# Input projections: the low part of every third weight tile made by ScalarE and an accumulating transfer instead of VectorE

## The chip, the core and the metric

The kernel runs on one core of one Trainium2 chip. The metric is device time in microseconds (us) of one execution. The engines are named as in the profile: PE is TensorE, PEld its weight loads, DVE VectorE, ACT ScalarE, POOL GpSimd, SP SyncE, which only issues transfers here.

## The reference, cut to what matters

The program is one encoder block over 256 tokens of 2048 channels. The change touches only the weights of the first product, `proj = h @ w_in`, and of that only the columns of the LRU branch and of the short convolution:

```
proj = jnp.einsum('bsd,dc->bsc', h, w_in)
lru_x, conv_x, conv_bg, conv_cg, g_lru, g_conv = jnp.split(proj, SPLIT_POINTS, axis=-1)
u = centred_dwconv(lru_x, lru_conv_w, lru_conv_b, LRU_CONV_LEFT)
...
v = centred_dwconv(conv_cg * conv_x, sc_conv_w, sc_conv_b, SHORT_CONV_LEFT)
```

All values are float32. `w_in` has 2048 rows and 12800 columns. `lru_x` takes the first 2560 columns, the three convolution inputs 2048 each, and the two gates `g_lru` and `g_conv` the last 4096. After that come two linear recurrences over the tokens, output products, a merge, a LayerNorm, an MLP of width 8192 and a second LayerNorm.

## The kernel before, in words

Every product is made in split precision. An operand is cut into a high part `hi`, which is the value cast to the type float32r that one pass of PE carries, and a low part `lo`, which is what the cast left over. With activations that are split likewise, the weight's high part meets both halves of the activations (one product over 512 columns, L137) and its low part the high half only (256 columns, L138). So one block of 128 by 128 weights costs two products, and a tile of eight blocks sixteen.

The weights come as tiles of 128 partitions by 1024 float32 (512 KB) in one long stream, `Weights`, in the order of their use. For each tile `load` does four things:

- it takes a raw buffer (tag `raw`, three of them) and a buffer each for `hi` and `lo` (six of each);
- SP issues the transfer from memory into `raw` (L85);
- ACT casts `raw` into `hi` (L66);
- DVE subtracts, `lo = raw - hi` (L67). This is the last reader of `raw`, so the raw buffer is free again behind it.

`take` keeps the stream up to five tiles ahead of the product that is emitted (`AHEAD = 5`). A scheduler then places the instructions of each engine in a fixed order. All engines run their own queue in that order, and a waiting instruction holds up what stands behind it in the same queue.

The input projections run in the order that the loop over the 20 heads at L531 writes down. For each head come one LRU block of columns (tiles named `l`, two per head), one gate product (tile `g`, half a tile, the recurrence's own weights) and two or three convolution blocks (tiles `c`, two each). Between them stands what is done with the products: L215 and L218 add the two halves of a PSUM bank, L258 and L260 are the LRU's convolution on DVE, L287 the gates' sigmoids on ACT, L289 and L309 two products of the recurrence on POOL, L304, L305 and L314 its exponentials, tangents and roots on ACT, L310 to L321 the rest of it with the scans on DVE. After the heads come the tiles `sg` of the two mixer gates, which have only L215, L218 and L367 behind them, and then the later layers.

Of the kernel before, what the change touches and what calls it, by code (L numbers as in the profile page):

```python
# [8 lines left out]
F32 = mybir.dt.float32  # L9
F32R = mybir.dt.float32r  # L10
AF = mybir.ActivationFunctionType
ALU = mybir.AluOpType
# [3 lines left out]
T = 256  # L16
# [21 lines left out]


class Job:  # L40
    """Weights' tiles that are taken from the stream, the products with them, and what is done with the products."""

    def __init__(self, specs, mm, post, chained=False):
        self.specs, self.mm, self.post, self.chained = specs, mm, post, chained
# [3 lines left out]
def block_kernel(ctx: ExitStack, tc: tile.TileContext, xT, x, par, w_in, w_gate, w_lru, w_conv, w_o, w1, w2,  # L48
                 ln1_g, ln1_b, b2, ln2_g, ln2_b, out):
    nc = tc.nc  # L50
# [7 lines left out]
    def bank_a(name):  # L58
        return psa.tile([P, 512], F32, tag="a", name=name)

    def bank_b(name):
        return psb.tile([P, 512], F32, tag="b", name=name)

    def split(raw, hi, lo):
        """raw = hi + lo, each with the mantissa that one pass of TensorE carries."""
        made = nc.scalar.copy(hi, raw)  # L66
        nc.vector.tensor_tensor(lo, raw, hi.bitcast(F32), op=ALU.subtract)  # L67
        return made

    class Weights:  # L70
        """All weights' tiles in the order of their use, loaded and split some tiles ahead of it."""

        def __init__(self):
            self.specs, self.tiles, self.taken = [], [], 0

        def alloc(self, name):
            raw = wp.tile([P, CH * P], F32, tag="raw", name=f"raw_{name}", bufs=3)
            hi = wp.tile([P, CH * P], F32R, tag="hi", name=f"hi_{name}", bufs=BUFS)
            lo = wp.tile([P, CH * P], F32R, tag="lo", name=f"lo_{name}", bufs=BUFS)
            return raw, hi, lo  # L80

        def load(self):
            src, n, name = self.specs[len(self.tiles)]
            raw, hi, lo = self.alloc(name)
            nc.sync.dma_start(raw[:, :n], src)  # L85
            split(raw[:, :n], hi[:, :n], lo[:, :n])
            self.tiles.append((hi, lo))

        def take(self, hold=False):
# [7 lines left out]
    stream = Weights()  # L97
# [5 lines left out]
        return par_sb[:, o : o + 1]  # L103

    def decay_scale():
        """-8 softplus(-lambda), with log1p by a Newton step on expm1(y) = 2 t / (1 - t), t = tanh(y / 2)."""
        n = 2 * HEADS
        o = PCOLS["lam"][0]
        lam = par_sb[:, o : o + n]
        tl = {k: cp.tile([P, n], F32, name=f"sp_{k}") for k in ("e", "y", "t", "r", "q")}  # L110
        e, y, t, r, q = (tl[k] for k in ("e", "y", "t", "r", "q"))
        c = cp.tile([P, n], F32, name="c_neg")
        cpos = cp.tile([P, n], F32, name="c_pos")
        nc.scalar.activation(e, lam, AF.Abs)
        nc.scalar.activation(e, e, AF.Exp, scale=-1.0)
        nc.scalar.activation(y, e, AF.Ln, bias=1.0)
        nc.scalar.activation(t, y, AF.Tanh, scale=0.5)
        nc.vector.tensor_scalar(r, t, -1.0, 1.0, op0=ALU.mult, op1=ALU.add)
        nc.vector.reciprocal(q, r)
        nc.vector.scalar_tensor_tensor(r, t, 2.0, q, op0=ALU.mult, op1=ALU.mult)  # L120
        nc.vector.tensor_tensor(t, r, e, op=ALU.subtract)
        nc.vector.tensor_scalar_add(q, e, 1.0)
        nc.vector.reciprocal(r, q)
        nc.vector.tensor_tensor(q, t, r, op=ALU.mult)
        nc.vector.tensor_tensor(r, y, q, op=ALU.subtract)
        nc.vector.tensor_scalar(t, lam, -1.0, 0.0, op0=ALU.mult, op1=ALU.max)
        nc.vector.tensor_tensor(y, t, r, op=ALU.add)
        nc.vector.tensor_scalar(c, y, -LRU_C, None, op0=ALU.mult)
        nc.vector.tensor_scalar(cpos, y, LRU_C, None, op0=ALU.mult)
        return c, cpos  # L130

    def mm_blocks(ps, hi, lo, k0, k, n, src, w0=0):
        """ps[:, :T] + ps[:, T:] = W.T @ (hi + lo): W's high part meets both parts, its low part the high one."""
        for i in range(k0, k0 + k):
            s = src(i)
            w = slice((i - k0 + w0) * P, (i - k0 + w0 + 1) * P)
            nc.tensor.matmul(ps, hi[:, w], s, start=i == 0, stop=False)  # L137
            nc.tensor.matmul(ps[:, :T], lo[:, w], s[:, :T], start=False, stop=i == n - 1)  # L138
# [12 lines left out]
        return Job(specs, mm, lambda: post(st["ps"]))  # L151

    def group_job(w, cs, nk, src, posts, name, after=None):
        """Some blocks of columns side by side, so that products can begin while their second operand is in the making."""
        st = {}
        cuts = [(k0, min(CH, nk - k0)) for k0 in range(0, nk, CH)]
        specs = [(w[c, :, k0 : k0 + k, :].rearrange("p k q -> p (k q)"), k * P, f"{name}{c}_{k0}") for k0, k in cuts for c in cs]

        def mm():
            st["ps"] = [bank_a(f"ps_{name}{c}") for c in cs]  # L160
            for k0, k in cuts:
                with tc.issue_after(after().ins) if after else nullcontext():
                    tiles = [stream.take() for _ in cs]
                for i in range(k):
                    for ps, (hi, lo) in zip(st["ps"], tiles):
                        mm_blocks(ps, hi, lo, k0 + i, 1, nk, src, i)

        def post():
            for ps, p in zip(st["ps"], posts):
                p(ps)  # L170

        return Job(specs, mm, post)

    def row_job(w, nk, src, post, name, tail=0, between=None):
        """Products with tokens on the output's partitions; over the last tiles one half of the tokens after the other."""
        st = {}
        n = nk // 2
        specs = [(w[i], 2 * 512, f"{name}_{i}") for i in range(n)]

        def products(ps, i, t, hi, lo):  # L180
            for kk in range(2):
                k = 2 * i + kk
                s = src(k)
                c = slice(kk * 512, (kk + 1) * 512)
                sh = s[:, t * P : (t + 1) * P]
                sl = s[:, T + t * P : T + (t + 1) * P]
                nc.tensor.matmul(ps[t], sh, hi[:, c], start=k == 0, stop=False)  # L187
                nc.tensor.matmul(ps[t], sh, lo[:, c], start=False, stop=False)  # L188
                nc.tensor.matmul(ps[t], sl, hi[:, c], start=False, stop=k == nk - 1)  # L189

        def mm():
            ps = st["ps"] = [bank_b(f"pr_{name}_{t}") for t in range(2)]
            for i in range(n - tail):
                hi, lo = stream.take()
                for t in range(2):
                    products(ps, i, t, hi, lo)
            last = [stream.take(between is not None and i > 2) for i in range(tail)]
            for t in range(2):
                for i, (hi, lo) in enumerate(last):
                    if t and between and i == tail - 1:  # L200
                        between()
                    products(ps, n - tail + i, t, hi, lo)
                if tail and not t:
                    post(ps[0], 0)

        def finish():
            for t in range(1 if tail else 0, 2):
                post(st["ps"][t], t)

        return Job(specs, mm, finish, chained=True)  # L210
# [13 lines left out]
        scope[name] = es = ExitStack()  # L224
        return es.enter_context(tc.tile_pool(name=name, bufs=1, reuse_waits="tile"))

    # x, channels on partitions, with the first weights among its parts
    xraw = sp.tile([P, KD, T], F32, tag="s0", name="xraw")
    xs = sp.tile([P, KD, 2 * T], F32R, tag="s1", name="xs")
    xsrc = lambda k: xs[:, k, :]  # L230
# [91 lines left out]
            d = hsrc(h)  # L322
            split(y[:, 0, :], d[:, :T], d[:, T:])

    # short convolution
    conv = {}
    cpads = []
    for i in range(2):
# [25 lines left out]
                split(s, conv["cs"][:, j, :T], conv["cs"][:, j, T:])  # L354
        return post

    # gates of the two mixers
    sg = {}

    def gate_sig_post(i):  # L360
# [6 lines left out]
            nc.scalar.activation(sg["s"][:, i, :], s, AF.Sigmoid)  # L367
        return post

    # the two mixers' outputs, merged  # L370
    mgd = {}

    def merge_post(j, part):
# [64 lines left out]
        return post  # L438

    def first_norm(t):  # L440
        """The normalized rows' transposes, scaled and shifted by channel, as the next products' second operand."""
        zp, z = zd["p"], zd["z"]
        if "hsp" not in zd:
            zd["hsp"] = sp.tile([P, KD, 2 * T], F32R, tag="s0", name="hsp")
# [1 line left out]
        for q in range(4):  # L446
            ps = (bank_b if t else bank_a)(f"tr{t}_{q}")
# [3 lines left out]
            for i in (0, 2):  # L451
# [5 lines left out]
                hi = hsp[:, js, t * P : (t + 1) * P]  # L457
# [72 lines left out]
    done = 2  # L530
    for h in range(HEADS):  # L531
# [7 lines left out]
        done = upto  # L539
# [7 lines left out]
    for c in range(4):  # L547
        jobs.append(row_job(w_o[c], KD, lambda k: mgd["m"][:, k, :], wo_post(c), f"o{c}", tail=5 if c == 3 else 0,
                            between=(lambda: first_norm(0)) if c == 3 else None))
    for half in range(2):  # L550
        f0 = half * HALF
        if not half:
            first = group_job(w1, list(range(3)), KD, lambda k: zd["hsp"][:, k, :], [ff_post(f) for f in range(3)], "f",
                              after=lambda: zd["normed"])
# [9 lines left out]
    for job in jobs:  # L564
        stream.specs += job.specs

    # the first tiles in small parts, x's among them
    cut = (2, 2, 4)
    first = [stream.alloc(s[2]) for s in stream.specs[:3]]
    k0 = 0  # L570
# [79 lines left out]
```

## Time and profile before

| what | value |
| --- | --- |
| median of 3 runs | 1651.99 us (1651.96 to 1653.0) |
| span of the profiled execution | 1649.8 us |
| PE busy in the span | 1614.6 us, 98% |
| DVE busy | 1064.8 us, 65% |
| ACT busy | 847.3 us, 51% |
| POOL busy | 64.2 us, 4% |
| granted PE clock, mean | 0.995 |
| tiles of 128 by 1024 named `c`, and named `l` | 92 and 38 |

The span runs from the first to the last instruction of the one execution that was profiled, and the page gives no other time of that execution; the runs' times contain what lies around the span. "Idle before" in a row of instructions is the time that the engine stood still just ahead of them, with the instruction that ended it. SPq is the queue in which SP issues transfers; its waits are waits of that queue, not of PE.

### The profile page before, as it was taken

Reading aid. Unit: us, or ns where it says so; the run is one execution under the profiler, and the core shown is the slowest. Engines: PE = TensorE matmul, PEld = TensorE weight load, DVE = VectorE, ACT = ScalarE, POOL = GpSimd, SP = SyncE. Lnnn points to the kernel's source line nnn. Section 1 sums busy time; section 2 is a strip of 40 time slices with the busy share of each in tenths; the row PEclk is TensorE's granted clock in tenths of the full one; section 3 lists DMA queues with packets and bytes.
Section 4 is the critical chain, followed back from the end, with each engine's and each line's share of the span. In section 5 each row is a group of like instructions: output and inputs, shape, how many; then the busy total and the mean of one; then the engine's idle time right before and its main releaser. Section 6 shows DMA issues by size and latency. Waiting matters only on the chain.

```text
span 1649.8 us, 22706 instructions
## 1 busy us (share of the span) xinstructions
PE 1614.6 (98%) x8592; PEld 1375.4 (83%) x8592; DVE 1064.8 (65%) x1437; ACT 847.3 (51%) x1215; POOL 64.2 (4%) x69
## 2 busy tenths in 40 slices
PE   7999999999999999999999899999999999999996
PEld 6888888888888888888888788888888888888885
DVE  5788888888865546666555777654444666654445
ACT  5676776676755544444333645443333445543331
POOL 0111111011100000000000000000000000000001
PEclk9999999999999999999999999999999999999998
DMA  7555555656566656665775556555565565565552
GB/s 231 188 172 187 192 173 185 188 170 190 175 203 204 194 178 186 192 190 181 246 254 167 165 186 202 188 192 183 187 191 184 187 190 189 189 236 191 183 188 89
DMA packets 88652, 312.05 MB, mean 189 GB/s; under 512 B 9824, under 2 KB 10720, under 8 KB 87648
## 3 DMA queue, kind: packets, MB, share of 16 engines
q1 hardware_dynamic: 87264, 302.75, 57.3%
q0 software_dynamic: 992, 7.34, 1.2%
q8 instruction: 67, 1.10, 0.3%
q10 hardware_dynamic: 288, 0.52, 0.1%
q14 instruction: 41, 0.34, 0.1%
HBM read 308.48 MB, written 2.10 MB: 188 GB/s over the span
## 4 chain that ended last, share of the span: by engine, by line
PE 71%; issue 13%; DVE 7%; DMA 4%; ACT 4%; POOL 0%; SPq 0%; ACTq 0%; POOLq 0%
PE ps_f L137 14%; PE ps_f L138 7%; PE ps_sg L137 6%; PE ps_c L137 5%; PE ps_yl L137 4%; PE pr_d L189 4%; PE pr_d L188 4%; PE pr_d L187 4%; PE ps_yc L137 4%; PE ps_sg L138 3%; PE ps_c L138 2%; PE ps_yl L138 2%; PE ps_yc L138 2%; PE ps_l L137 2%; DMA raw_l<-in_w_in 2%
## 5 line engine op out<-in xcount | busy, mean ns | idle before, releaser
L137 PE MATMUL ps_f<-hsp,hi_f 128*128 128x512 f32 x1024 | 358.6, 393 | 1.0 <-DVE hsp L459 1.0
L138 PE MATMUL ps_f<-hsp,lo_f 128*128 128x256 f32 x1024 | 286.4, 280 | 0.0
L67 DVE TENSOR_TENSOR lo_d<-raw_d,hi_d 128x1024 fp32r<-128x1024 f32 x128 | 156.7, 1225 | 183.7 <-ACT hi_d L66 183.7
L137 PE MATMUL ps_c<-xs,hi_c 128*128 128x512 f32 x736 | 259.4, 394 | 0.0
L66 ACT CAST hi_d<-raw_d 128x1024 fp32r<-128x1024 f32 x128 | 134.6, 1052 | 220.0 <-PE pr_d L189 193.8
L137 PEld LDWEIGHTS ps_f<-hsp,hi_f 128*128 128x128 f32 x1024 | 192.0, 187 | 47.2 <-ACT hf L455 1.3
L67 DVE TENSOR_TENSOR lo_f<-raw_f,hi_f 128x1024 fp32r<-128x1024 f32 x128 | 156.2, 1225 | 115.7 <-ACT hi_f L66 114.3
L66 ACT CAST hi_f<-raw_f 128x1024 fp32r<-128x1024 f32 x128 | 134.1, 1051 | 175.1 <-PE ps_f L137 138.9
L138 PE MATMUL ps_c<-xs,lo_c 128*128 128x256 f32 x736 | 207.5, 282 | 6.4 <-DVE lo_c L67 6.2
L189 PE MATMUL pr_d<-hi_d,ff 128*128 128x512 f32 x512 | 203.2, 397 | 0.0
L188 PE MATMUL pr_d<-lo_d,ff 128*128 128x512 f32 x512 | 203.2, 397 | 0.0
L187 PE MATMUL pr_d<-hi_d,ff 128*128 128x512 f32 x512 | 203.2, 397 | 0.0
L138 PEld LDWEIGHTS ps_f<-hsp,lo_f 128*128 128x128 f32 x1024 | 192.2, 188 | 0.0
L137 PE MATMUL ps_sg<-xs,hi_sg 128*128 128x512 f32 x512 | 179.4, 394 | 0.5 <-DVE sg L218 0.5
L137 PEld LDWEIGHTS ps_c<-xs,hi_c 128*128 128x128 f32 x736 | 138.0, 188 | 31.6
L138 PEld LDWEIGHTS ps_c<-xs,lo_c 128*128 128x128 f32 x736 | 138.3, 188 | 10.5 <-DVE lo_c L67 10.5
L138 PE MATMUL ps_sg<-xs,lo_sg 128*128 128x256 f32 x512 | 143.2, 280 | 0.0
L67 DVE TENSOR_TENSOR lo_c<-raw_c,hi_c 128x1024 fp32r<-128x1024 f32 x92 | 114.4, 1245 | 28.2 <-ACT hi_c L66 26.0
L66 ACT CAST hi_c<-raw_c 128x1024 fp32r<-128x1024 f32 x92 | 96.4, 1048 | 67.4 <-DMA raw_c<-in_w_in 63.6
L67 DVE TENSOR_TENSOR lo_sg<-raw_sg,hi_sg 128x1024 fp32r<-128x1024 f32 x64 | 78.7, 1233 | 67.8 <-ACT hi_sg L66 66.3
L189 PEld LDWEIGHTS pr_d<-hi_d,ff 128*128 128x128 f32 x512 | 96.6, 189 | 23.3
L187 PEld LDWEIGHTS pr_d<-hi_d,ff 128*128 128x128 f32 x512 | 96.6, 189 | 23.3
(165 smaller groups left out, 2789.5 us busy)
## 6 DMA issues: line engine op xcount, KB each, us to landing
raw_f<-in_w SPq DMA_DIRECT2D x128, 512.0 KB, 4.3
raw_d<-in_w SPq DMA_DIRECT2D x128, 512.0 KB, 3.3
raw_c<-in_w_in SPq DMA_DIRECT2D x92, 512.0 KB, 4.1
raw_sg<-in_w_in SPq DMA_DIRECT2D x64, 512.0 KB, 4.6
raw_l<-in_w_in SPq DMA_DIRECT2D x38, 512.0 KB, 4.6
raw_yl<-in_w_lru SPq DMA_DIRECT2D x32, 512.0 KB, 4.3
raw_yc<-in_w_conv SPq DMA_DIRECT2D x32, 512.0 KB, 3.8
raw_o<-in_w_o SPq DMA_DIRECT2D x32, 512.0 KB, 4.3
```

The lines of the kernel that those rows point to most:

```text
L66: made = nc.scalar.copy(hi, raw)
L67: nc.vector.tensor_tensor(lo, raw, hi.bitcast(F32), op=ALU.subtract)
L137: nc.tensor.matmul(ps, hi[:, w], s, start=i == 0, stop=False)
L138: nc.tensor.matmul(ps[:, :T], lo[:, w], s[:, :T], start=False, stop=i == n - 1)
L187: nc.tensor.matmul(ps[t], sh, hi[:, c], start=k == 0, stop=False)
L188: nc.tensor.matmul(ps[t], sh, lo[:, c], start=False, stop=False)
L189: nc.tensor.matmul(ps[t], sl, hi[:, c], start=False, stop=k == nk - 1)
```

## The change

In `load`, a tile is treated in another way if its name begins with `c` or `l` and its number in the stream leaves 1 when divided by three. ACT makes `hi` as before, and then a second instruction of ACT writes `-hi` into `lo`. No instruction of DVE takes part. The transfer that adds `raw` to `lo` in place is remembered in `rest`, and is issued from POOL's queue after the next tile's load, cast and subtraction have been emitted. With it `lo = -hi + raw`, and `raw` is free only when that transfer has landed.

```
         def load(self):
             src, n, name = self.specs[len(self.tiles)]
+            rest, self.rest = self.rest, None
+            if name[0] in "cl" and len(self.tiles) % 3 == 1:
+                raw, hi, lo = self.alloc(name)
+                nc.sync.dma_start(raw[:, :n], src)
+                nc.scalar.copy(hi[:, :n], raw[:, :n])
+                nc.scalar.mul(lo[:, :n], hi[:, :n].bitcast(F32), -1.0)
+                self.rest = lo[:, :n], raw[:, :n]
+                self.tiles.append((hi, lo))
+                return
             raw, hi, lo = self.alloc(name)
             nc.sync.dma_start(raw[:, :n], src)
             split(raw[:, :n], hi[:, :n], lo[:, :n])
+            if rest:
+                nc.gpsimd.dma_start(*rest, accum_op=ALU.add)
             self.tiles.append((hi, lo))
```

The rest of the diff splits `alloc` in two and removes docstrings and comments, which shifts line numbers: the loads are L99, and L92 where the tile is of the new kind; the new cast and negative of ACT are L93 and L94, the accumulating transfer L102. 44 tiles are of the new kind.

On SP the order of the loads is the same, but not what they wait for. These are the loads around the fourth head before. The names are the raw buffers with the scheduler's numbers; DMAHW is an earlier transfer of SP's, DVE the subtraction that frees the buffer, DMASW a transfer of POOL's.

```order
L85 DMA raw_c_2_8_809<-in_w_in 128x1024 [waits DMAHW5_49,DVE_49]
L85 DMA raw_c_3_0_836<-in_w_in 128x1024 [waits DMAHW6_49,DVE_49]
L85 DMA raw_c_3_8_858<-in_w_in 128x1024 [waits DMAHW7_49,DVE_49]
L85 DMA raw_l_0_888<-in_w_in 128x1024 [waits DMAHW0_49,DVE_49]
L85 DMA raw_l_8_920<-in_w_in 128x1024 [waits DMAHW1_49,DVE_49]
L85 DMA raw_g_942<-in_w_gate 128x512 [waits DMAHW2_49,DVE_49,Activation_49]
L85 DMA raw_c_3_0_971<-in_w_in 128x1024 [waits DMAHW3_49,DVE_49]
L85 DMA raw_c_3_8_993<-in_w_in 128x1024 [waits DMAHW4_49,DVE_49]
L85 DMA raw_c_3_0_1023<-in_w_in 128x1024 [waits DMAHW5_49,DVE_49]
```

The same nine loads on SP after the change; the rows at L92 are tiles of the new kind.

```order
L92 DMA raw_c_2_8_815<-in_w_in 128x1024 [waits DMAHW6_49,DVE_49]
L99 DMA raw_c_3_0_842<-in_w_in 128x1024 [waits DMAHW5_49,DMASW5_49]
L99 DMA raw_c_3_8_865<-in_w_in 128x1024 [waits DMAHW7_49,DVE_49]
L92 DMA raw_l_0_895<-in_w_in 128x1024 [waits DMAHW1_49,DVE_49]
L99 DMA raw_l_8_927<-in_w_in 128x1024 [waits DMAHW0_49,DMASW6_49]
L99 DMA raw_g_950<-in_w_gate 128x512 [waits DMAHW2_49,DVE_49]
L92 DMA raw_c_3_0_979<-in_w_in 128x1024 [waits DMAHW4_49,DVE_49]
L99 DMA raw_c_3_8_1001<-in_w_in 128x1024 [waits DMAHW5_49,DVE_49]
L99 DMA raw_c_3_0_1032<-in_w_in 128x1024 [waits DMAHW3_49,DMASW7_49]
```

Before, each load waited for a subtraction of DVE. Now every third one waits for an accumulating transfer. `raw_l_8_927` waits for the one that reads `raw_c_2_8_815`, four loads ahead of it, and `raw_c_3_0_1032` for the one that reads `raw_l_0_895`, five loads ahead. Over the whole program the distance is five loads 25 times, four 16 times and three 3 times.

POOL's queue at the same place before holds only the recurrence's products, of the heads 2 to 5:

```order
L309 TENSOR_TENSOR q_764<-a_754 128x512 [waits Activation_49]
L309 TENSOR_TENSOR q_767<-a_759 128x512 [waits DVE_49,Activation_49]
L289 TENSOR_TENSOR ri_964<-ri_964,u_695 128x512 [waits Activation_49]
L289 TENSOR_TENSOR ri_1147<-ri_1147,u_911 128x512 [waits DVE_49,Activation_49]
L309 TENSOR_TENSOR q_1163<-a_1153 128x512 [waits Activation_49,Pool_49]
L309 TENSOR_TENSOR q_1166<-a_1158 128x512 [waits DVE_49,Activation_49]
```

After the change the accumulating transfers of POOL stand between them (L289 is now L305, L309 is L325):

```order
L325 TENSOR_TENSOR q_773<-a_765 128x512 [waits DVE_49,Activation_49]
L102 DMA lo_c_2_8_817<-raw_c_2_8_815 128x1024 [waits DMAHW0_49,DMASW4_49,Activation_49]
L305 TENSOR_TENSOR ri_972<-ri_972,u_700 128x512 [waits Activation_49]
L102 DMA lo_l_0_897<-raw_l_0_895 128x1024 [waits DMASW5_49,DMAHW3_49,PE_49,Activation_49]
L102 DMA lo_c_3_0_981<-raw_c_3_0_979 128x1024 [waits DMASW6_49,DMAHW6_49,PE_49,Activation_49]
L305 TENSOR_TENSOR ri_1157<-ri_1157,u_918 128x512 [waits DVE_49,Activation_49]
L102 DMA lo_c_3_8_1056<-raw_c_3_8_1054 128x1024 [waits DMASW7_49,DMAHW1_49,PE_49,Activation_49]
L325 TENSOR_TENSOR q_1173<-a_1163 128x512 [waits Activation_49,Pool_49]
```

17 of the 44 transfers stand directly behind a product at L305, which waits for the sigmoids of a gate.

More of the change, by code (lines that the diff above doesn't have):

```diff
@@ L73, in __init__, with alloc_parts @@
         def __init__(self):
-            self.specs, self.tiles, self.taken = [], [], 0
+            self.specs, self.tiles, self.taken, self.rest = [], [], 0, None
         def alloc(self, name):
             raw = wp.tile([P, CH * P], F32, tag="raw", name=f"raw_{name}", bufs=3)
+            return raw, *self.alloc_parts(name)
+        def alloc_parts(self, name):
             hi = wp.tile([P, CH * P], F32R, tag="hi", name=f"hi_{name}", bufs=BUFS)
             lo = wp.tile([P, CH * P], F32R, tag="lo", name=f"lo_{name}", bufs=BUFS)
-            return raw, hi, lo
+            return hi, lo
         def load(self):
             src, n, name = self.specs[len(self.tiles)]
+            rest, self.rest = self.rest, None
[7 more added lines that the diff above has]
+                return
             raw, hi, lo = self.alloc(name)
```

## The prediction

> **What bounds the kernel now.** I read the page's list of engines first, for the span, and then busy time by stretch, for the stage that the change touches. The columns are the stretch, its length, and the busy time and number of instructions of PE, PEld, DVE, ACT and POOL.
>
> ```profile
> span 1649.8 us, 22706 instructions
> ...
> PE 1614.6 (98%) x8592; PEld 1375.4 (83%) x8592; DVE 1064.8 (65%) x1437; ACT 847.3 (51%) x1215; POOL 64.2 (4%) x69
> ```
>
> ```profile
> core 0: us, PE busy (x) PEld busy (x) DVE busy (x) ACT busy (x) POOL busy (x), PEclk, DMA share, GB/s
> ...
> 60.00:425.00 365.00, 357.70 (x2089) 311.55 (x2089) 311.04 (x468) 262.01 (x427) 42.93 (x35) 1.00 0.56 180
> 425.00:600.00 175.00, 173.79 (x995) 151.22 (x994) 103.92 (x126) 98.80 (x153) 5.18 (x4) 1.00 0.62 198
> ```
>
> PE sets the end: it is busy 98% of the span. From 60 to 425 us, the middle of the stage with the tiles `c` and `l`, PE is idle for 365.0 - 357.7 = 7.3 us. DVE is busy for 311 of 365 us there, 85%, and ACT for 262, 72%. So DVE is crowded in this stage, but PE loses almost nothing by it. Next come the waits between engines in the same stretch (total us, times, longest), and those of SP's queue.
>
> ```profile
> ACT hi_c L66 <- DMA raw_c<-in_w_in: 56.0, 47, 2.8
> ...
> ACT hi_l L66 <- DMA raw_l<-in_w_in: 21.0, 20, 2.8
> ...
> PE ps_c L138 <- DVE lo_c L67: 6.2, 7, 1.3
> ...
> ACT hi_c L66 <- PE ps_c L137: 1.4, 2, 0.9
> ...
> PE pg L280 <- DVE us L67: 0.9, 2, 0.6
> ```
>
> ```profile
> SPq L85 <- DVE lo_c L67: 95.6, 38, 4.5
> SPq L85 <- DVE us L67: 45.3, 14, 4.0
> SPq L85 <- DVE lo_l L67: 38.2, 18, 3.9
> SPq L85 <- DVE y L321: 36.9, 9, 4.3
> ```
>
> PE's small loss is waiting for low parts, 6.2 us, and 0.9 us for `us`. What matters more stands in the other rows. ACT's casts wait for the weights to land (56.0 + 21.0 us) and hardly for a free `hi` buffer (1.4 us). SP's queue waits for DVE to be through with a raw buffer: these four rows alone make 216 us of 365. So the stream doesn't run its full five tiles ahead here. It runs at the pace at which three raw buffers come round, and that pace just about feeds PE.
>
> How long one round takes can be added up. In the same stretch these are the transfers (count, size, median us from issue to landing) and the two steps on a landed tile (busy us, mean ns):
>
> ```profile
> raw_c<-in_w_in SPq DMA_DIRECT2D x82, 512.0 KB, 4.1
> raw_l<-in_w_in SPq DMA_DIRECT2D x34, 512.0 KB, 4.6
> raw_g<-in_w_gate SPq DMA_DIRECT2D x18, 256.0 KB, 3.2
> ```
>
> ```profile
> L67 DVE TENSOR_TENSOR lo_c<-raw_c,hi_c 128x1024 fp32r<-128x1024 f32 x82 | 102.2, 1248 | 23.4 <-ACT hi_c L66 21.1 <-PE ps_c L138 1.1 <-PE ps_l L137 0.7
> ...
> L66 ACT CAST hi_c<-raw_c 128x1024 fp32r<-128x1024 f32 x83 | 87.0, 1048 | 59.8 <-DMA raw_c<-in_w_in 56.0 <-PE ps_c L137 1.4 <-PE ps_l L137 1.4
> ```
>
> 82 + 34 + 18 = 134 tiles in 365 us are 2.72 us per tile. A raw buffer takes one tile in three, so it comes round every 8.2 us. Its work is a landing of 4.2 (between the rows), the cast's 1.05 and the subtraction's 1.25: 6.5 us. The other 1.7 us are queueing on ACT and DVE.
>
> **The change, part by part.** *DVE* loses 44 subtractions of 1.25 us, 55 us. In the stage its share falls from 85% to about 71%. As it isn't the bound, this is worth at most PE's idle time, 7.3 us, and it shortens the queueing of the other tiles. I take 1.0 us instead of 1.7 for an ordinary pass from now on: 7.5 us in all.
>
> *ACT* gains 44 negatives of 128 by 1024. No such row exists; the cast of the same shape, 1.05 us, is the nearest. That is 46 us, 72% to about 84% of the stage, still off the path by itself.
>
> *POOL* gains 44 issues, and *the transfer* takes the place of the subtraction as the last reader of the raw buffer. POOL's own transfers before are far larger, but they are the only rows of that queue. First come the two late ones of 1 MB each, with the ns that the issue takes on POOL and the us until they land; they are issued back to back, so the first lands after 7.6 us and the second after 10.8. The last row is a median over two landings of such transfers.
>
> ```profile
> L494 POOL DMA_DIRECT2D cst<-in_ln_g x1: 582/582/582, 1456.6 to 1456.6; - x1
> L494 POOL DMA_DIRECT2D cst<-in_ln_b x1: 528/528/528, 1457.2 to 1457.2; - x1
> ...
> DMA to landing us min/median/max: 7.6/9.2/10.8
> ```
>
> ```profile
> cst<-in_ln_b POOLq DMA_DIRECT2D x2, 1024.0 KB, 11.0
> ```
>
> An issue takes 0.53 to 0.58 us of POOL, say 0.6. The landing is the one large unknown. The adding transfer writes 512 KB and must read both `raw` and `lo`, 1 MB. From below it is bounded by the plain 512 KB load, 4.1 us. From above I take 11.0 us, the median of the last row, where each 1 MB transfer shares the queue with others. The nearest row is one 1 MB transfer on that queue beside the weights, 7.6 us; mine is a little under it, 7 us, as less is written. A gain is excluded by the lower row alone: 4.1 us stand where 1.25 stood. [...]
>
> So a pass of a raw buffer with a tile of the new kind costs 4.2 + 1.05 + 1.05 + 0.6 + 7 and 0.8 of queueing on ACT and POOL: 14.7 us. The queueing on POOL is real, since 17 of the transfers stand behind a product that waits for a gate's sigmoids. What the longer pass does depends on who gets the buffer next, and the order shows that.
> - Distance five, 25 times: the load five places on takes the buffer, then the one seven on, then the one nine on, which is of the new kind again. Nine tiles take 7.5 + 7.5 + 14.7 = 29.7 us where PE wants them in 9 x 2.72 = 24.5. That is 5.2 us for three new tiles, 1.73 each, 43 us.
> - Distance four, 16 times: an ordinary tile and then a new one. Six tiles take 7.5 + 14.7 = 22.2 us against 16.3. That is 5.9 for two, 2.95 each, 47 us.
> - Distance three, 3 times: 14.7 against 8.2, 6.5 each, 20 us.
>
> The sum is 110 us. Five tiles of lead don't hide it: a lead covers a delay once, not a pace that is too slow for 130 tiles. SP's queue is in order, so a load that waits for the adding transfer also holds up those behind it. Nothing gives the time back later, as PE is at 98% everywhere else. The profiled span becomes 1649.8 + 110 = 1760. The runs' median stands 2.2 us above that span, so I say 1762 us.
>
> The ends come from the same sum. With 4.1 us for the transfer and no queueing at all the passes are 6.5 and 11.0. Distance five then costs nothing (24.0), distance four 0.6 each, distance three 2.8: 18 us, 1670. With 11.0 us and the old 1.7 us of queueing on every pass they are 8.2 and 19.6. That makes 3.8, 5.75 and 11.4 each: 95 + 92 + 34 = 221 us, 1873.
>
> **The rivals.**
> *Faster.* If the raw buffers had slack that the trace doesn't show, the change would only relieve DVE, and PE's 7.3 us of idle time would go: 1645 us. It decides at the landing time: by the two longer rings without any queueing (24.5 - 13.0 - 6.9 and 16.3 - 6.5 - 6.9) the transfer would have to land within 4.6 and 2.9 us. For it speaks the share of DVE, 85%; against it the 216 us of SP's waits and the row of 4.1 us. Chance 0.05.
> *No change.* The gain on DVE and the longer rings cancel, with a transfer near 4 us: 1652. Chance 0.04.
> *The transfer is slow.* If the addition itself sets the pace, at 20 us say, beyond every row here, a new pass takes 27.7 us. The rings give 6.1, 9.45 and 19.5 each: 152 + 151 + 59 = 362 us, 1649.8 + 362 + 2.2 = 2014. For it speaks only that no row shows an adding transfer; against it that the transfer engines are busy 0.56 of this stage and could take more. Chance 0.11.
>
> **How the numbers follow.** The forecast has 0.80 and lies between 1670 and 1873. I end the range at 1900 to take in the mildest of the slow transfers. A measurement of this kernel tells about 0.2% from no change, 3.3 us. Only the first rival is faster by more, 0.05, and only the second within it, 0.04. All else is slower, 0.91.
>
> **What would show each step.** In the profile after, PE should be idle for about 110 us more, all before the tiles `sg`, with waits of L138 that end in a transfer into `lo_c` or `lo_l`. SP's queue should wait for those transfers, and DVE should fall to about 70% or less in that stage. The transfers' row should show about 7 us to landing. The forecast is wrong if they land in 7 us and PE still doesn't wait, for then the rings are not what feeds PE; if they land far from 7 us, only the size is wrong.

## The result and the profile after

The changed kernel takes 1728.41 us (median of 4 runs, 1726.6 to 1730.66), beside 1651.97 us for the kernel before (4 runs, 1650.55 to 1653.0). The ratio is 1.0465, with a 95% interval from 1.0451 to 1.0479. It is 76.4 us slower. The page after begins so; the last line is the transfer queue of POOL, with its packets, MB and share of the transfer engines; before it had 1.2%.

```profile
span 1725.3 us, 22766 instructions
...
PE 1640.4 (95%) x8592; PEld 1393.8 (81%) x8592; DVE 1016.8 (59%) x1393; ACT 889.7 (52%) x1259; POOL 103.9 (6%) x113
...
q0 software_dynamic: 7328, 30.41, 8.4%
```

The span grew by 75.5 us, from 1649.8 to 1725.3. PE's idle time in it rose from 1649.8 - 1614.6 = 35.2 us to 84.9, by 50 us. The other 26 us are PE being *busy* longer on the same 8592 products. Where this happened is told by the first product of the tiles `sg`. Their row before, and then after, gives the ns of one product (least, median, most) and the us of the first and last start.

```profile
L137 PE MATMUL ps_sg<-xs,hi_sg x512: 390/393/470, 435.4 to 615.1; 128*128 128x512 f32 x171
```

```profile
L153 PE MATMUL ps_sg<-xs,hi_sg x512: 391/393/398, 509.4 to 688.2; 128*128 128x512 f32 x171
```

509.4 - 435.4 = 74.0: all but 1.5 us of the growth lies ahead of `sg`, in the stage that the change touches. This is that stage after, from 60 to 425 us, with the columns of the row in the prediction.

```profile
60.00:425.00 365.00, 322.54 (x1786) 277.94 (x1785) 230.34 (x364) 256.45 (x400) 68.50 (x64) 0.95 0.73 205
```

In the same 365 us PE does less, 1786 recorded products instead of 2089. DVE is down to 63% of the stage and ACT is at 70%. The transfer engines went from 0.56 to 0.73 of it, and PE's granted clock from 1.00 to 0.95. Next stand all the waits of PE in this stretch, and then the first rows of SP's queue.

```profile
PE ps_c L154 <- DMA lo_c<-raw_c: 28.7, 13, 7.8
PE ps_l L154 <- DMA lo_l<-raw_l: 13.0, 7, 3.9
PE ps_c L154 <- DVE lo_c L67: 0.6, 1, 0.6
```

```profile
SPq L99 <- DMA lo_c<-raw_c: 51.0, 22, 6.8
SPq L92 <- DMA raw_c<-in_w_in: 50.6, 18, 4.8
SPq L92 <- DVE lo_c L67: 31.6, 11, 4.4
SPq L99 <- DMA lo_l<-raw_l: 24.1, 9, 6.1
```

PE waits almost only for the low parts that the transfers make. SP waits for the same transfers, 75 us, before it can load again. SP's second row, the waits for `raw_c`, belongs to a buffer that comes round too: the load at 237.88, for instance, stands until 235.46, when a tile that was loaded from 229.63 on has landed, and then until 237.86, when DVE has subtracted that tile. Two stories fit these rows, and the experiments have to tell them apart: the low part comes late for PE, or the raw buffer comes late for the next load. The transfers' own rows in the stretch (count, size, median us to landing), and the lines of L102 over the whole program (ns of an issue on POOL, then landing times), are these:

```profile
raw_c<-in_w_in SPq DMA_DIRECT2D x71, 512.0 KB, 4.6
raw_l<-in_w_in SPq DMA_DIRECT2D x30, 512.0 KB, 4.5
lo_c<-raw_c POOLq DMA_DIRECT2D x23, 512.0 KB, 5.0
lo_l<-raw_l POOLq DMA_DIRECT2D x10, 512.0 KB, 5.7
...
raw_g<-in_w_gate SPq DMA_DIRECT2D x16, 256.0 KB, 3.7
```

```profile
L102 POOL DMA_DIRECT2D lo_c<-raw_c x31: 849/865/1045, 30.2 to 497.8; - x31
...
DMA to landing us min/median/max: 4.5/5.1/8.3
```

The adding transfer lands in 5.1 us, and the 0.87 us of its issue lie inside that time. The ring of the raw buffer can be read off the chain that ended last (start, length, what):

```profile
207.88 5.90 DMA lo_l<-raw_l
...
213.79 5.90 DMA raw_c<-in_w_in
...
219.77 1.06 ACT hi_c L66
...
220.85 1.23 DVE lo_c L67
...
229.63 5.83 DMA raw_c<-in_w_in
...
236.50 1.05 ACT lo_c L94
...
237.84 6.96 DMA lo_c<-raw_c
```

The transfer lands at 213.78, and the load that waited for its raw buffer starts at 213.79. Behind it come cast, subtraction, the next load, a negative, and the next adding transfer. Between the subtraction at 220.85 and the load at 229.63, where the rows are left out, the chain runs through DVE's and ACT's work for the recurrence and the next tiles, so queueing is part of this ring.

### The profile page after: what moved, and what is told of

It is laid out like the page before. It is cut to its first block, busy times and chain, and to the rows that moved or that the text cites. A ratio compares the mean times of both kernels' runs of the same rounds, so it can differ in the third digit from the quotient of the medians.

```text
span 1725.3 us, 22766 instructions
## 1 busy us (share of the span) xinstructions
PE 1640.4 (95%) x8592; PEld 1393.8 (81%) x8592; DVE 1016.8 (59%) x1393; ACT 889.7 (52%) x1259; POOL 103.9 (6%) x113
## 3 DMA queue, kind: packets, MB, share of 16 engines
q0 software_dynamic: 7328, 30.41, 8.4%
## 4 chain that ended last, share of the span: by engine, by line
PE 64%; DMA 16%; issue 12%; ACT 4%; DVE 3%; POOL 0%; SPq 0%; POOLq 0%; ACTq 0%; DVEq 0%
PE ps_f L153 14%; PE ps_f L154 7%; PE ps_sg L153 7%; DMA raw_c<-in_w_in 7%; PE ps_yl L153 4%; DMA lo_c<-raw_c 4%; PE ps_sg L154 3%; PE pr_d L204 3%; PE pr_d L205 3%; PE pr_d L203 3%; PE ps_yc L153 3%; PE ps_c L153 2%; PE ps_yl L154 2%; DMA raw_l<-in_w_in 2%; PE ps_yc L154 2%
## 5 line engine op out<-in xcount | busy, mean ns | idle before, releaser
L153 PE MATMUL ps_c<-xs,hi_c 128*128 128x512 f32 x736 | 271.0, 407 | 0.0
L154 PE MATMUL ps_c<-xs,lo_c 128*128 128x256 f32 x736 | 213.9, 291 | 40.5 <-DMA lo_c<-raw_c 39.8
L154 PEld LDWEIGHTS ps_c<-xs,lo_c 128*128 128x128 f32 x736 | 144.7, 197 | 47.6 <-DMA lo_c<-raw_c 46.2
L153 PEld LDWEIGHTS ps_c<-xs,hi_c 128*128 128x128 f32 x736 | 144.1, 196 | 33.0
L204 PEld LDWEIGHTS pr_d<-lo_d,ff 128*128 128x128 f32 x512 | 96.5, 188 | 23.4
L153 PEld LDWEIGHTS ps_sg<-xs,hi_sg 128*128 128x128 f32 x512 | 95.9, 187 | 23.0
```

## The experiments

Each edit is against the changed kernel except where it says before. Each ratio is against runs of the kernel before on the same chip.

### Is it the buffer that is held, or the low part that comes late?

**e4_other_target.** The transfer still reads `raw` and still holds it, but it adds into a buffer that no product of this stage reads. The products read `hi` in place of the low part.

```
+                k = len(self.tiles) // 3 % 2 * 2
+                other = hs2[:, k : k + 2, :].rearrange("p a b -> p (a b)")
-                nc.scalar.mul(lo[:, :n], hi[:, :n].bitcast(F32), -1.0)
-                self.rest = lo[:, :n], raw[:, :n]
-                self.tiles.append((hi, lo))
+                nc.scalar.mul(other, hi[:, :n].bitcast(F32), -1.0)
+                self.rest = other, raw[:, :n]
+                self.tiles.append((hi, hi))
```

> The changed kernel, but ACT's negative and the transfer go to a spare part of another tile, and PE reads the high part in place of the low part of these tiles, so it leaves out their low part; the raw buffer is still held until the transfer lands, but PE waits for no transfer. Theory A (round of the raw buffers): 1715 to 1740 us, with PE waiting for casts and loads instead. Theory B (chain too long for the lead): PE's waits are gone, 1640 to 1665 us. Theory C (traffic): 1715 to 1740 us.

Measured: 1729.42 us, 1.0454 (1.0439 to 1.047). That is the time of the changed kernel, although PE waits for no transfer any more. Its first waits in the same stretch are now others:

```profile
PE ps_c L155 <- ACT hi_c L66: 11.8, 9, 2.8
PE ps_c L156 <- DVE lo_c L67: 10.4, 10, 2.2
PE ps_c L155 <- ACT hi_c L93: 8.6, 7, 3.0
```

So the 42 us that PE spent waiting for `lo_c` and `lo_l` named what came last and not what cost the time. While the raw buffers are held, the late low part adds nothing.

**e3_other_source.** The reverse: PE waits for the transfer as in the change, but the transfer adds the activations `xs`, so that `raw` is free after the cast.

```
-                self.rest = lo[:, :n], raw[:, :n]
+                self.rest = lo[:, :n], xs[:, 0:2, :].rearrange("p a b -> p (a b)").bitcast(F32)
```

> The changed kernel, but the transfer adds the first two blocks of the activations (a tile that nobody writes in this stage) to the low part instead of the raw tile, so the low part is a wrong number; negative, transfer and PE's wait for it stay, and the raw buffer is free behind the cast. Theory A (round of the raw buffers): the hold is gone, 1640 to 1665 us. Theory B (chain too long for the lead): PE waits for the same transfers as before, 1715 to 1735 us. Theory C (traffic): 1715 to 1735 us.

Measured: 1695.9 us, 1.0254 (1.0223 to 1.0284). Giving the buffer back early saves 32 us of the loss, and 43 us stay. The hold isn't all of it.

**e5_own_buffer.** Every third tile, all tiles of the new kind among them, takes one raw buffer that is kept for these tiles, and the others share the two that are left. The excerpt leaves out the same argument for the other tiles of that third and for the first three tiles. The distance from a new tile to the load that waits for it becomes three everywhere.

```
-        def alloc(self, name):
-            raw = wp.tile([P, CH * P], F32, tag="raw", name=f"raw_{name}", bufs=3)
+        def alloc(self, name, tag="raw", bufs=2):
+            raw = wp.tile([P, CH * P], F32, tag=tag, name=f"raw_{name}", bufs=bufs)
...
-                raw, hi, lo = self.alloc(name)
+                raw, hi, lo = self.alloc(name, "rawn", 1)
```

> The changed kernel, but every third tile has one raw buffer to itself and the other two thirds share two, so that the new tiles always wait for the transfer of the one three tiles before. Theory A: a new pass of 13.6 us stands against 8.2 us for three tiles, 5.4 us for each of 44 tiles, 237 us more than before the change: 1840 to 1900 us. Theory B and theory C: chain and traffic are the same as in the changed kernel, 1715 to 1740 us.

Measured: 1910.56 us, 1.1548 (1.1529 to 1.1567). No work is added and no memory taken away; the buffers are only handed out in another order, and the loss more than triples. Three rows of its transfers in the stretch:

```profile
raw_c<-in_w_in SPq DMA_DIRECT2D x51, 512.0 KB, 4.4
...
lo_c<-raw_c POOLq DMA_DIRECT2D x16, 512.0 KB, 7.2
lo_l<-raw_l POOLq DMA_DIRECT2D x7, 512.0 KB, 6.2
```

A pass with a new tile is here 4.4 + 1.05 + 1.06 + 6.9 + 0.8 = 14.2 us (6.9 is the mean of the last two rows by their counts, 0.8 the prediction's queueing), where 3 x 2.72 = 8.2 are to be had. 6.0 x 44 = 264 us, against 258 measured. Timed on the trace, from the load's start to the transfer's landing, the 23 new passes of the stretch take 14.4 us on average, which would be 273 us. Both workings lie within 6% of the measurement, so the pace of the ring sets the time here. The time itself is 10 us above theory A's range, whose pass of 13.6 us was too short although it counted the issue twice, once as 0.87 and once inside the landing of 5.2.

### What the transfers cost when they hold nothing

**e7_traffic_only.** Both of the edits above: the transfer adds `xs` into `hs2`, nothing waits for it and it holds no raw buffer. The negatives stay.

```
+                self.rest = other, xs[:, 0:2, :].rearrange("p a b -> p (a b)").bitcast(F32)
+                self.tiles.append((hi, hi))
```

> The changed kernel with all its negatives and transfers, but each transfer adds the first blocks of the activations to a spare part of another tile, so it holds no raw buffer and PE waits for none; PE reads the high part in place of the low part of these tiles, which leaves out their low part. Theory A, now as the hold of the raw buffer plus the wait of PE that was left at 1696 us when the hold alone was gone: 1645 to 1665 us. Theory C (traffic takes the time from the loads): what was left without the hold stays, 1685 to 1705 us.

Measured: 1691.35 us, 1.0218 (1.0194 to 1.0243). About half of the loss is there without any hold. From here to e4_other_target, which only adds the hold, it is 38 us more. From here to e3_other_source, which only adds PE's wait, it is 4.5 us, and the runs of the two overlap (1684.8 to 1694.18 here, 1688.77 to 1701.5 there), so no cost of that wait is shown.

**e10_traffic_no_negative** and **e11_hold_no_negative.** All tiles are cast and subtracted as before, and the 44 transfers run beside that; in the second they read `raw` and hold it. A copy of two columns on DVE puts each transfer behind its tile's subtraction. The sums land in `hs2`, the outputs of the last four heads, and change what a later product reads there.

```
-                nc.scalar.copy(hi[:, :n], raw[:, :n])
-                nc.scalar.mul(lo[:, :n], hi[:, :n].bitcast(F32), -1.0)
-                self.rest = lo[:, :n], raw[:, :n]
...
+                split(raw[:, :n], hi[:, :n], lo[:, :n])
+                nc.vector.tensor_copy(other[:, 0:2], lo[:, 0:2])
+                self.rest = other, xs[:, 0:2, :].rearrange("p a b -> p (a b)").bitcast(F32)
```

In e11_hold_no_negative the last line is `self.rest = other, raw[:, :n]`. What the excerpt leaves out picks `other` as in e4_other_target and sets `hs2` to zero beforehand.

> The kernel with DVE's subtraction for every tile as before the change and no negative on ACT, and in addition 44 adding transfers of 512 KB beside it, from the activations into a spare part of another tile; nothing waits for them but the next one, and they hold no raw buffer (DVE copies two columns per transfer so that it starts when it does in the changed kernel). Theory E: the traffic alone, 1660 to 1672 us. Theory C: 1685 to 1695 us. Theory D: 1650 to 1658 us.

> The same as the kernel with DVE's subtraction and 44 transfers beside it, but each transfer reads the raw tile, so that the raw buffer is held until it lands; no negative on ACT, and PE waits for no transfer. Theory A, the round of the raw buffers with a pass of 4.6 + 1.05 + 1.25 + 0.1 + 0.87 + 5.2 + 0.8 = 13.9 us, as long as in the changed kernel: 1715 to 1740 us. Theory E, where ACT's negatives cost 25 us apart from the hold: 1695 to 1710 us.

Measured: 1690.21 us, 1.0234 (1.0211 to 1.0258), and 1749.55 us, 1.0599 (1.0559 to 1.064). The first is the kernel before with the traffic added, besides the small copies, and it loses 38.6 us. The loads land later:

```profile
raw_c<-in_w_in SPq DMA_DIRECT2D x76, 512.0 KB, 4.6
hs<-xs POOLq DMA_DIRECT2D x36, 512.0 KB, 6.5
raw_l<-in_w_in SPq DMA_DIRECT2D x32, 512.0 KB, 5.3
raw_g<-in_w_gate SPq DMA_DIRECT2D x16, 256.0 KB, 5.3
```

Weighted by their counts the loads land in 4.87 us. By the rows of before it was 4.11. The `c`, `l` and `g` tiles are 92 + 38 + 20 = 150, so each of the three raw buffers makes 50 passes, and 50 x 0.76 = 38 us. By this working the traffic too is paid on the raw buffers: it makes every pass longer, and not only those with a new tile. The same working for e7_traffic_only starts from loads of 5.31 us (its rows are 5.1, 6.0 and 4.9 us for `c`, `l` and `g`, weighted by 75, 32 and 16) and takes off the subtraction that the 44 new tiles don't wait for there, (150 x 1.20 - 44 x 1.25) / 3 = 42 us against 37.9 measured. That is agreement and not proof: no run has this traffic beside a fourth raw buffer in the kernel before. The second kernel adds the hold on top, 59 us more, and is 10 us above theory A's range. That it costs more than the changed kernel may be because DVE's subtraction stands in the held time as well and DVE keeps all its work; no run isolates it.

**e8_half.** The transfer adds only the first half of a tile's `raw`, so the second half of these low parts stays `-hi`.

```
-                self.rest = lo[:, :n], raw[:, :n]
+                self.rest = lo[:, : n // 2], raw[:, : n // 2]
```

> The changed kernel, but the transfer adds only the first half of the raw tile, so half of the low part of these tiles is left as the negative. The scheduler places more of the loads four behind the transfer they wait for (36 of 44, and 6 three behind). Theory A: with 4.0 us to landing a new pass is 12.4 us, which costs 1.8 us at distance four and 4.2 at distance three, 65 + 25 = 90 us: 1725 to 1750 us, no better than the whole transfer. Theory C (traffic): half of the bytes, half of the loss, 1685 to 1695 us.

Measured: 1712.31 us, 1.0358 (1.0343 to 1.0374). Half the bytes land in 4.0 us in the stretch, so most of the hold stays. The result lies between the two theories' numbers, as a cause of two parts would have it.

### Is it the negative?

**e9_negative_only.** No transfer at all, so `raw` is never added and these low parts stay `-hi`.

```
-                self.rest = lo[:, :n], raw[:, :n]
```

> The changed kernel without the transfers: the 44 low parts stay the negatives of the high parts, so the raw tile is never added. No hold, no traffic, DVE relieved of 44 subtractions, ACT with 44 negatives more. Theory E, the loss is a sum of hold (1728 - 1691 = 37 us), negatives (about 25, by the 1678 us of the kernel that adds on DVE) and traffic (the rest, about 14): 1670 to 1680 us. Theory D, all that is left without the hold is ACT: 1685 to 1695 us. Theory C, all of it is traffic: 1640 to 1655 us.

Measured: 1644.59 us, 0.9956 (0.9941 to 0.9971). The row of the stretch:

```profile
60.00:425.00 365.00, 362.58 (x2143) 318.95 (x2143) 263.32 (x442) 304.71 (x479) 43.41 (x36) 1.00 0.56 185
```

ACT's busy time rises to 83% of the stage, and yet the kernel is 7.0 us faster than before. Two things help here at once and are not told apart: DVE's relief, and raw buffers that come free behind the cast for these tiles. As long as nothing holds the buffer, no cost of the negatives is seen.

**e12_dve_negative.** The negative on DVE in place of ACT.

```
-                nc.scalar.mul(lo[:, :n], hi[:, :n].bitcast(F32), -1.0)
+                nc.vector.tensor_scalar(lo[:, :n], hi[:, :n].bitcast(F32), -1.0, None, op0=ALU.mult)
```

> The changed kernel with the negative on DVE in place of ACT, transfer and hold as they are; more of the loads stand four behind the transfer that they wait for (28, and 5 three behind). Theory E: ACT's 25 us go, 1695 to 1710 us. Theory A: the pass is the same and the distances are shorter, 1725 to 1750 us.

Measured: 1728.19 us, 1.0468 (1.044 to 1.0495), the time of the change. No cost of having the negative on ACT is seen. The test isn't clean, since the distances are shorter here, which by the rings costs time, while DVE's negative is shorter, which saves some: DVE runs 31 instructions more in the stretch than in the change and is busy 20.2 us longer (250.6 and 230.3), about 0.65 us each, an estimate, against 1.06 on ACT.

**e6_dve_add.** The negative stays on ACT, and DVE adds `raw`, with no transfer.

```
-                nc.gpsimd.dma_start(*rest, accum_op=ALU.add)
+                nc.vector.tensor_tensor(rest[0], rest[1], rest[0].bitcast(F32), op=ALU.add)
```

> The changed kernel with its negative on ACT, but DVE adds the raw tile to the low part at the place where the transfer was issued; no transfer is left. Theory A (round of the raw buffers) and theory C (traffic) both say that the loss goes with the transfer: 1648 to 1668 us, since the pass of such a tile is longer than before by the negative, 1.06 us, alone. Theory D, ACT's 44 negatives and the casts that queue behind them are the cost: 1700 to 1730 us.

Measured: 1678.41 us, 1.0154 (1.0136 to 1.0173), about 10 us above what was expected. The addition stands where the transfer's issue stood, in the order behind the next tile's subtraction. So it waits for that tile to land too, and `raw` is held all that time. In one piece of the chain a load lands at 98.62, a subtraction on DVE takes 99.78 to 101.01, and an addition starts behind it at 101.40; SP's queue waits 76 us in the stretch, 23 times, for these additions. That explains the miss as an argument; no run isolates it. As a test of the transfer alone this kernel is therefore not clean.

### Does a fourth raw buffer bring it back?

**e1_raw4**, and **e2_before_raw4**, which is the same edit in the kernel before. Every fourth tile of the stage takes a raw buffer of its own.

```
+            if name[0] in "clg" and len(self.tiles) % 4 == 3:
+                raw = lp.tile([P, CH * P], F32, tag="rawx", name=f"raw_{name}", bufs=1)
+            else:
+                raw = wp.tile([P, CH * P], F32, tag="raw", name=f"raw_{name}", bufs=3)
```

> The changed kernel with a fourth raw buffer in the stage of the tiles c, l and g (every fourth tile takes it). Theory A, the raw buffers' round is what feeds PE: with four buffers twelve tiles hold two ordinary passes of 7.5 us and one new pass of 4.6 + 1.05 + 1.06 + 0.87 + 5.2 + 0.8 = 13.6 us, 28.6 us against the 32.7 us that PE takes for twelve tiles, so nearly all of the 76 us goes: 1645 to 1665 us. Theory B, the low part is late because the chain cast, negative, transfer is longer than the lead of five tiles: the chain is the same, 1715 to 1735 us. Theory C, the added traffic of the transfers slows the loads: the traffic is the same, 1715 to 1735 us.

> The kernel before the change with a fourth raw buffer in the stage of the tiles c, l and g. If the round of the raw buffers is what PE's 7.3 us of idle time in this stage come from (theory A), they go: 1643 to 1648 us. If they come from DVE's crowded queue alone, nothing changes: 1651 to 1654 us.

Measured: in the kernel before 1639.49 us (1639.34 to 1639.77), 0.9918 (0.9903 to 0.9933), better than was expected. In the stretch PE is busy throughout:

```profile
60.00:425.00 365.00, 365.00 (x2162) 321.71 (x2160) 322.52 (x486) 269.06 (x443) 44.34 (x36) 1.00 0.57 188
```

This is the fastest kernel of the study. It also shows that the three raw buffers were what held PE's last 7 us in this stretch.

In the changed kernel the same edit gives 1724.01 us, 1.0423 (1.0406 to 1.044), only 4 us better, where the ring alone would have given it nearly all back. This was a miss. These are SP's first waits there in the stretch, and a piece of the chain:

```profile
SPq L102 <- DMA lo_c<-raw_c: 82.5, 24, 8.0
SPq L102 <- DMA lo_l<-raw_l: 44.1, 9, 8.5
```

```profile
238.18 0.09 POOL q L328
238.27 5.84 issue
244.13 7.62 DMA lo_c<-raw_c
251.79 0.58 PE ps_c L157
```

The buffer is still what the loads wait for, 127 us instead of 75. The hold has grown: the median landing of an adding transfer is 6.7 us over the whole program (4.5 to 10.6), instead of 5.1. And the transfer can leave late: in the piece shown POOL is through with its product at 238.27, and the transfer is issued 5.8 us later. What it waits for is ACT. Its tile's cast (L96), its negative (L97) and the issue are these:

```profile
240.89 1.03 ACT L96 CAST hi_c<-raw_c 128x1024 fp32r<-128x1024 f32 x1
242.78 1.05 ACT L97 ACTIVATE lo_c<-hi_c 128x1024 fp32r<-128x1024 f32 x1
244.13 0.87 POOL L105 DMA_DIRECT2D lo_c<-raw_c  x1 [4.91 <-ACT hs L66]
```

That tile had landed at 232.95 and waited 7.9 us for its cast. Until 240.9 ACT is busy without a gap, most of the time with the recurrence's sigmoids, exponentials and roots (L306, L323, L324, L333), which its fixed order puts ahead of the cast. POOL's order costs nothing: each of the 44 transfers starts within 0.4 us of the end of its negative, here and in the changed kernel alike.

Timed on the trace from the load's start to the transfer's landing, the pass of a new tile in the stretch has grown from 13.5 us in the changed kernel to 17.5 here, on average: the load from 4.5 to 5.7, the wait for the cast from 0.4 to 2.0, the adding transfer from 5.7 to 6.9. An ordinary pass went from 7.6 to 9.9. Twelve tiles then take 2 x 9.9 + 17.5 = 37.3 us of a buffer, more than the 32.7 that PE wants, so the ring of four is as full as the ring of three was. What this doesn't settle is which came first. In the kernel before with a fourth buffer an ordinary pass takes 10.5 us and PE waits for nothing, so a part of the longer passes is only loads that run ahead.

## Why the prediction was right, and where its sizes were off

The forecast, slower by the pace of the raw buffers, came out; its size was 110 us where 76.4 were measured. The hold that it named is there, but it is about half of the loss. The other half is traffic, which the prediction put at nothing, and a landing that it put too long made up for that, which is luck. By its steps:

- **The bound before** was read rightly: a fourth raw buffer alone takes PE to 365.00 busy of 365 (e2_before_raw4), and without transfers the kernel gains 7.0 us (e9_negative_only), where the bound for DVE's relief was 7.3.
- **The negatives** take 1.06 us each, as forecast, and no cost of them shows where nothing holds the buffer (e9_negative_only). In the change they stand inside the held time, as one term of the new pass, and there they count: 1.06 of the 12.5 us below.
- **The transfer's landing** is the term that was too large. It was put at 0.6 + 7 us, and it is 5.1 in the median, 5.7 on average in the stretch, issue included. The 0.6 was counted twice, since the 7.6 us that it was taken from run from the issue's start. The 1 MB of reads that it was reckoned with is the author's estimate, and no run shows it: POOL's queue has 30.41 MB after and 7.34 before, 0.52 MB for each of the 44, so the page counts a transfer's 512 KB once.
- **The loads' landing** was kept at 4.2 us and left out a cost. The added transfers take the transfer engines from 0.56 to 0.73 of the stage, and the loads land later. In the changed kernel it is 4.45 us, weighted by the counts in its rows, and in e10_traffic_no_negative 4.87. The prediction put all of the loss on the hold; traffic that holds nothing costs 38.6 us by itself.
- **The queueing on POOL** was called real, since 17 transfers stand behind a product that waits for sigmoids. It isn't: all 44 transfers start within 0.4 us of the end of their negative. The queueing of a new pass is on ACT, 0.4 us before the cast and 0.4 before the negative on average, so with the 0.3 up to the issue it is 1.1 us, where 0.8 was put.
- **The rings** held. With 4.5 for a load, 5.1 for the transfer and the prediction's queueing, an ordinary pass takes 4.5 + 1.05 + 1.25 + 1.0 = 7.8 us and a new one 4.5 + 1.05 + 1.06 + 5.1 + 0.8 = 12.5. Distance five: (28.1 - 24.5) / 3 x 25 = 30. Distance four: (20.3 - 16.3) / 2 x 16 = 32. Distance three: (12.5 - 8.2) x 3 = 13. The sum is 75 us. That it agrees so closely is partly luck, as it takes the median landings and the prediction's queueing. With the averages of the trace, 7.6 and 13.5 us, the same sum is 35 + 38 + 16 = 89 us, 13 too much. e5_own_buffer, with distance three only, is the harder test, at 264 against 258. And with a fourth buffer the rings foretold nearly no loss from fixed passes, where the passes grew and the loss stayed (e1_raw4): the sum tells the pace for passes that are known, and a pass changes with what runs beside it.
- **What would show it**: the idle time was to grow by 110 us and grew by 50, since part of the loss came as slower products (below). The waits of the low parts' products did end in the transfers, but e4_other_target shows that this sign proves little: without those waits the time is the same. SP's waits for the transfers were the sign that counted. DVE fell to 63%, where about 70% or less was forecast.

The 76 us are so made up of traffic and hold in about equal parts: 38 us for e7_traffic_only, which has DVE's relief in it, and 38 more for the hold (e4_other_target). PE's own wait for the low part adds nothing beside the hold, and no more than the scatter of the runs where nothing is held (e3_other_source). The parts don't simply add, though. With DVE's work kept the same hold costs 59 us (e10_traffic_no_negative to e11_hold_no_negative), and the adding transfer takes 7.9 us in the stretch in e7_traffic_only, against 5.0 and 5.7 in the change, so the two kernels are not alike in the rest.

## What to carry to other kernels

Before a step is moved to an idle engine or queue, ask which buffer it holds and how many such buffers there are: the longer hold costs its excess over (buffers or distance) x (pace), on every pass, however idle the engine is. Here POOL was busy 6% of the span, and in e5_own_buffer that sum gave 264 us where 258 were measured. A transfer also had a price here beside its own time, since the loads landed in 4.87 us beside it instead of 4.11 (e10_traffic_no_negative); count that on every pass of the ring that they feed. One more buffer need not bring it back: it gave about 4 us of 76 here, since the passes grew with it. And a wait row names who came last: before believing it, take that wait away by itself and see whether the time moves. Here PE's 42 us of waits for the transfers went, and the kernel took 1729.42 us beside 1728.41 (e4_other_target).

## What the runs showed of the hardware

From 60 to 425 us of the changed kernel PE's granted clock reads 0.50 in eight places, in windows of 1 us, each in or behind a stop of PE of 2.2 to 7.8 us. These are stretches on PE alone (length, busy, products, clock, share of the transfer engines, GB/s), around one of its waits for `lo_c`:

```profile
237.00:244.80 7.80, 2.32 (x17) 0.98 0.75 179
244.80:248.00 3.20, 3.15 (x10) 0.52 0.73 209
248.00:252.00 4.00, 4.00 (x24) 1.00 0.85 207
```

PE stood for 5.5 us there, from 239.3 to 244.85. Over the 3.2 us in the second row the clock was 0.52, and a product of 512 columns took 0.63 us instead of 0.39; in the third row it was 1.00. This is where the 26 us of longer busy time belong: the mean clock of the span is 0.995 before and 0.978 after, and 0.017 of 1725 us is 29 us, an estimate. In the stretch it is 1.00 before, 0.95 after and, in e5_own_buffer where PE waits most, 0.86.

```profile
60.00:425.00 365.00, 273.85 (x1287) 225.71 (x1288) 163.28 (x262) 178.54 (x284) 47.50 (x46) 0.86 0.53 147
```

Where the raw buffers set the pace a slower product may only fill time that PE would have waited; whether the slower clock adds to the total was not isolated.

The landing of the adding transfer is not one number: its median is 5.1 us in the change, 6.7 with a fourth raw buffer, and 7.9 where it reads `xs` (e3_other_source). Whether what it reads or what runs beside it makes the difference, no run separates. Half the bytes still take 4.0 us in the stretch.
